# Neighbourhood attention: position biases added by VectorE together with the row maximum, instead of by matmuls with the identity

## The chip, the core and the metric

The kernel runs on one core of a Trainium2 chip. Its engines have a queue each: TensorE (PE in the profile; PEld is its weight load), VectorE (DVE), ScalarE (ACT), GpSimd (POOL) and SyncE (SP), which issues most of the DMA transfers. Each executes its own list of instructions in order and waits on semaphores for the others. The metric is the time of one execution on the device in microseconds (us); three runs of the kernel before took 1873.71, 1877.98 and 1898.75 us, so the median is 1877.98 us.

## The reference

Two network blocks run one after the other on 256 tokens of width 1024. The second block projects its input for three mixers (a gated linear recurrence, called hgrn in the code, a delta-rule recurrence, called rwkv, and a neighbourhood attention, called na), joins them by an output projection, and ends with a mixture of 32 experts. Only the attention is touched by the change. Cut to what matters, with 8 heads of 64 channels, 256 latent tokens on a grid of 4 rows by 64 columns, and 256 context tokens:

```python
s_win = jnp.einsum('bhjqd,bhrjkd->bhjqrk', q_row, k_blk) * scale
bias = rpb[:, row_idx[None, None, :, None], col_idx[:, :, None, :]]
s_win = jnp.where(in_win[:, :, None, :], s_win + bias, NEG_INF_2)
s_ctx = jnp.einsum('bhjqd,bhld->bhjql', q_row, kc_h) * scale
s_all = jnp.concatenate([s_win.reshape(s_win.shape[:4] + (n_win,)), s_ctx], axis=-1)
prob = jax.nn.softmax(s_all, axis=-1)
o = (jnp.einsum('bhjqrk,bhrjkd->bhjqd', p_win, v_blk)
     + jnp.einsum('bhjql,bhld->bhjqd', p_ctx, vc_h))
```

A query sees the latent keys in its window, with a bias by relative position, and all context keys without one. The softmax runs over both together.

## The kernel before, in words

The attention of the latent tokens is `na_lat`. It goes in eight steps (j, i): j is one of four pairs of heads, i one of two halves of the 256 queries. The two heads of a pair lie in rows 0 to 63 and 64 to 127 of the tiles `q`, `k` and `kc`, so that a matmul of one head uses half of the array's rows (64*128 in the profile). For each step and head (`par`) a PSUM tile `sj` of 128 queries by 512 keys is made: 256 latent keys (L1478) and 256 context keys (L1481). The pool of `sj` has two buffers (`LPS`, L25), which the projections before the attention use too.

The bias of a head, window mask included, was prepared much earlier in device memory (`na_table`). `na_bias` (L1403) loads it with four strided transfers on SP's queue (L1409) into a tile `nab`, of which there are two, so that the tile of head n is that of head n+2. It is added in PSUM by a matmul with the identity as the stationary operand and the bias as the moving one (L1475), ahead of the head's own matmuls. Then DVE takes the negative maximum of the 512 sums (L1485), ACT the exponentials with their sum (L1487), DVE the reciprocal (L1488), ACT the scaling (L1489). `flip` transposes the probabilities on PE (L1498) and ACT copies them out (L1499); after both halves of a pair, `values` multiplies them with the values (L1510, L1512).

The work around it is written as generators, taken in turns by `lat_mix` (L1576): the end of hgrn (L1007 scores, L1062 to L1069 read-out), two groups of rwkv (L1229 to L1366, among them the rounds L1289, L1290, L1294, L1296, L1298, L1299 between PE and DVE), and the attention. From what is written a scheduler in the compiler's front end sets the order of each engine by its own estimates, so that a change in one place moves instructions on several engines. SP's list in this part is: the loads `nkl` and `nvl` of the context keys and values, the biases of heads 0 to 3, four rows of the output projection `wo`, an expert weight, the biases of heads 4 to 7, and then the other expert weights (L1774), each into a buffer that older work has to give up. After the attention its pools are closed, and their space becomes expert buffers (L1624 to L1630). The output projection (L366 to L368 into `so`), the router and the 32 experts (L1928 to L1972) follow.

## Time and profile before

| | |
|---|---|
| runs | 1873.71, 1877.98, 1898.75 us; median 1877.98 us |
| the profiled execution | 1878.12 us, its span 1876.3 us |
| mean granted TensorE clock | 0.958 of full speed |
| busy share of the span | PE 92%, DVE 58%, ACT 37%, POOL 8% |
| matmuls with the identity (L1475) | 32 instructions, two for each of 16 tiles, between 1265.8 and 1360.3 us |
| attention of the latent tokens | from 1265.8 us to its last ACT copy at 1371.5 us |
| last stretch with experts | DMA engines at 425 GB/s from 1440 to 1860 us |

An f32 matmul of the program stands as two instructions in the trace. [...] The profile models the ends of matmuls, so a duration of one is its latency; what it takes of PE's time is read from the chain of waits, where each piece runs until the next one starts.

### The profile page before, as it was taken

The numbers are of one execution on the slowest core, as the hardware profiler recorded it, in microseconds if no ns is written. First come the engines' busy times: TensorE is split into PE (matmuls) and PEld (weight loads), VectorE is DVE, ScalarE is ACT, GpSimd is POOL, SyncE is SP. The second block draws the span as 40 slices with busy tenths as digits, with TensorE's granted clock in tenths as the row PEclk, the third lists the DMA queues.
The fourth block names the chain that finished last, engine by engine and source line by source line (L and its number), as shares of the span: only waits on it lengthen the run. The fifth ranks groups of instructions, "written<-read, shape, count | busy, mean of one in ns | idle before, by whom it ended". The sixth has DMA issues, their size and how long they took to land.

```text
span 1876.3 us, 37673 instructions
## 1 busy us (share of the span) xinstructions
PE 1726.2 (92%) x15846; PEld 1476.6 (79%) x15846; DVE 1096.1 (58%) x2087; ACT 691.3 (37%) x1078; POOL 149.5 (8%) x295
## 2 busy tenths in 40 slices
PE   7999999999989999999999978989988888887876
PEld 6879999999988889999999978976777555544443
DVE  5558578998645466689996589884544111111111
ACT  3356445654433355555553336422532000000000
POOL 2600000000220000000000001120001100101000
PEclk9999999999999999999999979975998999988999
DMA  9855555555677867444443433320349999999997
GB/s 311 250 205 165 169 192 186 190 175 214 211 226 266 289 226 224 150 166 146 159 157 124 149 146 124 113 68 12 113 187 373 428 429 427 429 429 428 429 428 290
DMA packets 94705, 441.14 MB, mean 235 GB/s; under 512 B 23796, under 2 KB 26388, under 8 KB 81728
## 3 DMA queue, kind: packets, MB, share of 16 engines
q1 hardware_dynamic: 90496, 432.17, 62.3%
q0 software_dynamic: 2224, 5.19, 1.2%
q8 instruction: 126, 2.06, 0.4%
q10 hardware_dynamic: 1808, 1.30, 0.2%
q14 instruction: 51, 0.42, 0.1%
HBM read 429.40 MB, written 9.20 MB: 234 GB/s over the span
## 4 chain that ended last, share of the span: by engine, by line
PE 55%; DMA 19%; DVE 7%; issue 2%; ACT 1%; POOL 1%; SPq 0%; ACTq 0%; POOLq 0%; DVEq 0%
PE g L366 8%; PE g L368 8%; PE g L367 8%; DMA we<-in_w_exp_up 6%; DMA we<-in_w_exp_gate 4%; DMA we<-in_w_exp_down 4%; PE g L1948 3%; PE acc L1972 2%; PE acc L368 2%; PE acc L366 2%; PE acc L367 2%; DVE wl L360 2%; DMA w<-in_w_in 1%; PE g L1965 1%; DMA z<-in_na_rpb 1%
## 5 line engine op out<-in xcount | busy, mean ns | idle before, releaser
L360 DVE TENSOR_TENSOR wl<-w,wh 128x1024 fp32r<-128x1024 f32 x347 | 429.2, 1238 | 234.9 <-ACT wh L359 230.4
L359 ACT ACTIVATE wh<-w 128x1024 fp32r<-128x1024 f32 x347 | 366.7, 1059 | 476.8 <-PE g L367 214.0
L366 PE MATMUL g<-xg,wh 128*128 128x256 f32 x1472 | 417.6, 284 | 13.2 <-ACT wh L359 13.2
L368 PE MATMUL g<-xg,wl 128*128 128x256 f32 x1472 | 416.8, 283 | 4.1 <-DVE wl L360 3.8
L367 PE MATMUL g<-xg,wh 128*128 128x256 f32 x1472 | 414.1, 281 | 0.0
L366 PEld LDWEIGHTS g<-xg,wh 128*128 128x128 f32 x1472 | 279.7, 190 | 19.8 <-ACT wh L359 13.8
L368 PEld LDWEIGHTS g<-xg,wl 128*128 128x128 f32 x1472 | 279.6, 190 | 13.8 <-DVE wl L360 5.8
L367 PEld LDWEIGHTS g<-xg,wh 128*128 128x128 f32 x1472 | 279.9, 190 | 4.2 <-issue 2.7
L1948 PEld LDWEIGHTS g<-we,xt 128*32 128x32 f32 x4096 | 109.9, 110 | 42.1 <-issue 27.9
L1948 PE MATMUL g<-we,xt 128*32 128x128 f32 x4096 | 125.9, 274 | 11.7 <-DMA we<-in_w_exp_up 11.7
L1954 DVE SCALAR_TENSOR_TENSOR hd<-hd,g 128x128 f32<-128x128 f32 x32 | 9.2, 288 | 214.0 <-ACT hd L1953 214.0
L1972 PE MATMUL acc<-dn,S 128*128 128x512 f32 (+1 forms) x264 | 123.2, 600 | 0.0
L1969 DVE TENSOR_TENSOR dn<-g,g2r 128x512 f32<-128x512 f32 (+1 forms) x66 | 44.6, 676 | 92.4 <-PE g L1965 90.2
L1965 PE MATMUL g<-we,ht 128*32 128x512 f32 (+1 forms) x528 | 71.4, 663 | 25.4 <-DMA we<-in_w_exp_down 16.7
L1953 ACT ACTIVATE hd<-g 128x128 f32<-128x128 f32 x32 | 8.9, 277 | 209.9 <-PE g L1948 209.9
L1972 PEld LDWEIGHTS acc<-dn,S 128*128 128x128 f32 x264 | 48.0, 197 | 43.4 <-issue 42.0
L1937 POOL TENSOR_SCALAR gr<-G,comb 128x128 f32<-128x128 f32 x64 | 38.1, 606 | 495.1 <-PE g L1941 351.9
L1943 ACT ACTIVATE S<-g 128x256 f32<-128x256 f32 x32 | 12.3, 384 | 156.2 <-PE g L1941 156.2
L366 PE MATMUL sj<-hl,wh 128*128 128x256 f32 x200 | 58.5, 292 | 6.8 <-ACT wh L359 5.7
L368 PE MATMUL sj<-hl,wl 128*128 128x256 f32 x200 | 57.8, 290 | 1.5 <-DVE wl L360 1.5
L367 PE MATMUL sj<-hl,wh 128*128 128x256 f32 x200 | 58.4, 292 | 0.1
L1965 PEld LDWEIGHTS g<-we,ht 128*32 128x32 f32 x528 | 15.9, 117 | 53.3 <-issue 37.4
(803 smaller groups left out, 3604.6 us busy)
## 6 DMA issues: line engine op xcount, KB each, us to landing
w<-in_w_in SPq DMA_DIRECT2D x135, 512.0 KB, 3.5
we<-in_w_exp_gate SPq DMA_DIRECT2D x32, 2048.0 KB, 37.3
we<-in_w_exp_up SPq DMA_DIRECT2D x32, 2048.0 KB, 38.4
we<-in_w_exp_down SPq DMA_DIRECT2D x31, 2048.0 KB, 34.3
w<-in_w_up SPq DMA_DIRECT2D x88, 512.0 KB, 3.3
wa<-in_w_ada SPq DMA_DIRECT2D x48, 512.0 KB, 4.9
w<-in_w_down SPq DMA_DIRECT2D x44, 512.0 KB, 3.3
w<-in_w_v SPq DMA_DIRECT2D x24, 512.0 KB, 3.4
```

The costliest lines, as they stand in the source:

```text
L359: s.nc.scalar.activation(hi, t, AF.Copy)
L360: s.nc.vector.tensor_tensor(lo, t, hi, op=OP.subtract)
L366: mm(out, w[0], x[0], start=first, stop=False, skip_group_check=sk)
L367: mm(out, w[0], x[1], start=False, stop=False, skip_group_check=sk)
L368: mm(out, w[1], x[0], start=False, stop=last, skip_group_check=sk)
L1937: nc.gpsimd.tensor_scalar(gr[:, i], G[:, i, e % 4, None, :].to_broadcast([128, 4, 32]), s.comb[:, i, e:e + 1], None, op0=OP.mult)
L1943: nc.scalar.activation(S, p[:, :T], AF.Copy)
L1948: nc.tensor.matmul(p[32 * j:32 * j + 32, q * 128:(q + 1) * 128], xt[:, k, (e % 4) * 32:(e % 4) * 32 + 32], w[:, k, j * 128:(j + 1) * 128], ...
L1954: nc.vector.scalar_tensor_tensor(hd[:, 0], hd[:, 0], 1.0, p[:, 0:128], op0=OP.add, op1=OP.mult)
L1965: nc.tensor.matmul(p[32 * c:32 * c + 32, :w], ht[:, c * 32:(c + 1) * 32], wd[:, c, q * w:(q + 1) * w], start=True, stop=True, tile_positio ...
L1969: nc.vector.tensor_tensor(dn, p[:, :w], s.g2r[:, q * w:(q + 1) * w], op=OP.mult)
L1972: nc.tensor.matmul(y[i][q * w // 512][:, o:o + w], S[:, i * 128:(i + 1) * 128], dn, start=(more and e == 0), stop=(e == 31), skip_group_ch ...
```

## The change

The bias tile gets three parts of 256 columns: bias of the first query half, zeros (a memset on POOL), bias of the second half. A step of the first half reads parts 0 and 1, a step of the second half parts 1 and 2; so for the second half the context keys are put ahead of the latent ones in PSUM, and the transposes pick their columns accordingly. The identity matmuls are gone. In their place the former maximum becomes one DVE operation that reads PSUM and the bias, writes the negative sum to the SBUF tile `e`, and keeps its minimum. ACT takes the exponentials from `e` instead of from PSUM. The bias loads are issued for both heads of a pair ahead of any matmul of the step, and the matmuls are written so that the two heads alternate.

```diff
--- before.py
+++ after.py
@@ -1401,12 +1401,14 @@
                 yield
 
     def na_bias(s, hd, pp):
-        b = pp.tile([128, 2, T], F32, name="nab", tag="nab", bufs=2)
+
+        b = pp.tile([128, 3, T], F32, name="nab", tag="nab", bufs=2)
+        s.nc.gpsimd.memset(b[:, 1], 0.0)
         base = s.nasc
         for qr in range(4):
             src = bass.AP(tensor=base.tensor, offset=base.offset + hd * 64 * 889 + (3 - qr) * 127 + 63,
                           ap=[[888, 64], [127, 4], [1, 64]])
-            s.nc.sync.dma_start(b[(qr % 2) * 64:(qr % 2) * 64 + 64, qr // 2].rearrange("p (r c) -> p r c", r=4), src)
+            s.nc.sync.dma_start(b[(qr % 2) * 64:(qr % 2) * 64 + 64, qr // 2 * 2].rearrange("p (r c) -> p r c", r=4), src)
         return b
 
     def na_qk(s, h, t0, gain, mul, rope, out):
@@ -1469,22 +1471,21 @@
             i0 = slice(i * 128, (i + 1) * 128)
             ps = [s.psj() for _ in range(2)]
             for par in range(2):
-                hd = 2 * j + par
                 if i == 0:
-                    nab[hd] = s.na_bias(hd, pp)
-                nc.tensor.matmul(ps[par][:, :T], s.ident, nab[hd][:, i], start=True, stop=False, skip_group_check=True)
+                    nab[2 * j + par] = s.na_bias(2 * j + par, pp)
+
+            for x, c in ((k, i), (kc, 1 - i)):
+                for par in range(2):
+                    r = half(par)
+                    nc.tensor.matmul(ps[par][:, c * T:c * T + T], q[r, j, i0], x[r, j], start=True, stop=True,
+                                     skip_group_check=True)
             for par in range(2):
-                r = half(par)
-                nc.tensor.matmul(ps[par][:, :T], q[r, j, i0], k[r, j], start=False, stop=True, skip_group_check=True)
-            for par in range(2):
-                r = half(par)
-                nc.tensor.matmul(ps[par][:, T:], q[r, j, i0], kc[r, j], start=False, stop=True, skip_group_check=True)
-            for par in range(2):
-                p = ps[par]
                 st = pp.tile([128, 4], F32, name="st", tag="st", bufs=2)
-                nc.vector.tensor_reduce(st[:, 0:1], p, axis=AX.X, op=OP.max, negate=True)
                 e = pp.tile([128, 512], F32, name="e", tag="e", bufs=3)
-                nc.scalar.activation(e, p, AF.Exp, bias=st[:, 0:1], accum_out=st[:, 1:2])
+
+                nc.vector.tensor_tensor_reduce(e, ps[par], nab[2 * j + par][:, i:i + 2].rearrange("p a t -> p (a t)"),
+                                               -1.0, 3e38, OP.add, OP.min, accum_out=st[:, 0:1])
+                nc.scalar.activation(e, e, AF.Exp, scale=-1.0, bias=st[:, 0:1], accum_out=st[:, 1:2])
                 nc.vector.reciprocal(st[:, 2:3], st[:, 1:2])
                 nc.scalar.activation(e, e, AF.Copy, scale=st[:, 2:3])
                 es[par, i] = e
@@ -1495,7 +1496,8 @@
                 pts[2 * j + par] = pp.tile([128, 4, T], F32, name="npt", tag="npt", bufs=3)
             p = s.ps2()
             for c in range(4):
-                nc.tensor.transpose(p[:, c * 128:(c + 1) * 128], e[:, c * 128:(c + 1) * 128], s.ident)
+                o = (c ^ 2 * i) * 128
+                nc.tensor.transpose(p[:, c * 128:(c + 1) * 128], e[:, o:o + 128], s.ident)
             nc.scalar.activation(pts[2 * j + par][:, :, i * 128:(i + 1) * 128], p.rearrange("p (c t) -> p c t", c=4),
                                  AF.Copy)
 
```

On each engine the order changes from the start of the attention to the output projection. The memsets stand on POOL as eight instructions: two before the last `hxs` and `hxp`, one ahead of the two `rgml` memsets, five behind them. SP's list is the same.

PE, the start of the attention (`nab` with `small` is the identity matmul; `nk` and `nkl` are the latent and the context keys, `hT` the queries; `rZl`, `rU` belong to rwkv, `ql` and `ye` to hgrn). Before:

```order
L1314 MATMUL sr<-rvtl,rgml_13362 128x64 x2
L901 MATMUL sx<-small,ye 128x128 x4
L1007 MATMUL sx<-ql,kl 128x128 x8
L1325 MATMUL sr<-rZl_14077,rRl_13459 128x64 x2
L1325 MATMUL sr<-rZl_14087,rRl_13471 128x64 x2
L1007 MATMUL sx<-ql,kl 128x128 x4
L1331 MATMUL sr<-rU1l_14302,rgml_13351 128x64 x2
L1007 MATMUL sx<-ql,kl 128x128 x4
L1331 MATMUL sr<-rU0l_14308,rgml_13362 128x64 x2
L1475 MATMUL sj<-nab,small 128x256
L1478 MATMUL sj<-nk,hT 128x256
L1481 MATMUL sj<-nkl,hT 128x256
```

Now:

```order
L1314 MATMUL sr<-rvtl,rgml_13362 128x64 x2
L1480 MATMUL sj<-nk,hT 128x256 x2
L901 MATMUL sx<-small,ye 128x128 x4
L1007 MATMUL sx<-ql,kl 128x128 x8
L1325 MATMUL sr<-rZl_14077,rRl_13459 128x64 x2
L1480 MATMUL sj<-nkl,hT 128x256 x2
L1325 MATMUL sr<-rZl_14087,rRl_13471 128x64 x2
L1007 MATMUL sx<-ql,kl 128x128 x4
L1331 MATMUL sr<-rU1l_14302,rgml_13351 128x64 x2
L1007 MATMUL sx<-ql,kl 128x128 x4
L1331 MATMUL sr<-rU0l_14308,rgml_13362 128x64 x2
```

The latent keys' matmuls of the first two heads now stand next to each other and ahead of L901, which waits for `ye`; the context keys' follow together, and no bias stands between them.

PE, the end of the first pair (`rbrl` is rwkv's, L1062 to L1069 the read-out of hgrn, L1498 and L1500 the transposes of the attention). Before:

```order
L1360 MATMUL sr<-rgml_13362,rU0l_14308 64x128
L1478 MATMUL sj<-nk,hT 128x256
L1481 MATMUL sj<-nkl,hT 128x256
L1062 MATMUL sx<-hf_13113,hS_115 128x256
L1251 MATMUL sr<-rbrl_14500,ranl_14501 128x256 x2
L1498 MATMUL sx<-small,e 128x128 x3
L1063 MATMUL sx<-hf_13114,hS_116 128x256
L1069 MATMUL sx<-hsc,hv 64x128
L1069 MATMUL sx<-hxc_14851,hv 64x128
```

Now:

```order
L1360 MATMUL sr<-rgml_13362,rU0l_14308 64x128
L1480 MATMUL sj<-nk,hT 128x256
L1480 MATMUL sj<-nkl,hT 128x256
L1251 MATMUL sr<-rbrl_14500,ranl_14501 128x256 x4
L1062 MATMUL sx<-hf_13113,hS_115 128x256
L1500 MATMUL sx<-small,e 128x128 x4
L1063 MATMUL sx<-hf_13114,hS_116 128x256
L1069 MATMUL sx<-hsc,hv 64x128
L1069 MATMUL sx<-hxc_14849,hv 64x128
```

The key matmuls of head 2 (L1480 at the top) have come ahead of L1251 and L1062, behind which they stood before, and four L1251 now stand in a row.

DVE, from the second half of the third pair to the first half of the last (`rTl`, `rRl`, `rY5l` are rwkv's). Before:

```order
L1485 TENSOR_REDUCE st<-sj 128x1
L1298 TENSOR_TENSOR rTl_14702<-sr,rTl_14702 128x16x16
L1299 TENSOR_TENSOR rRl_14670<-sr,rRl_14670 128x16x16
L1488 RECIPROCAL st<-st 128x1
L1485 TENSOR_REDUCE st<-sj 128x1
L1290 TENSOR_TENSOR rY5l_15109<-sr,consts_79 128x512
L1488 RECIPROCAL st<-st 128x1
L1290 TENSOR_TENSOR rY5l_15116<-sr,consts_79 128x512
L1485 TENSOR_REDUCE st<-sj 128x1
L1298 TENSOR_TENSOR rTl_14695<-sr,rTl_14695 128x8x32
L1299 TENSOR_TENSOR rRl_14658<-sr,rRl_14658 128x8x32
L1488 RECIPROCAL st<-st 128x1
```

Now:

```order
L1486 ISA e,st<-sj,nab 128x512
L1486 ISA st 128x1
L1298 TENSOR_TENSOR rTl_14702<-sr,rTl_14702 128x16x16
L1299 TENSOR_TENSOR rRl_14670<-sr,rRl_14670 128x16x16
L1489 RECIPROCAL st<-st 128x1
L1290 TENSOR_TENSOR rY5l_15105<-sr,consts_79 128x512
L1486 ISA e,st<-sj,nab 128x512
L1486 ISA st 128x1
L1486 ISA e,st<-sj,nab 128x512
L1486 ISA st 128x1
L1290 TENSOR_TENSOR rY5l_15112<-sr,consts_79 128x512
L1489 RECIPROCAL st<-st 128x1
```

Each maximum is now the new operation with the bias as an operand, followed by a row that reads its minimum out. Those of head 5's second half and head 6's first half (the second and third L1486 with an input) now stand next to each other.

## Rows read from the trace of the kernel before

**Rows 1.** The page, part 1: busy time, share of the span, instructions

```profile
PE 1726.2 (92%) x15846; PEld 1476.6 (79%) x15846; DVE 1096.1 (58%) x2087; ACT 691.3 (37%) x1078; POOL 149.5 (8%) x295
```

**Rows 2.** Windows: length, busy time (instructions) per engine, PEclk, DMA share, GB/s

```profile
1256.40:1307.60 51.20, 51.20 (x176) 35.92 (x174) 23.63 (x51) 8.39 (x19) 4.90 (x4) 0.50 0.18 41
1307.60:1372.00 64.40, 64.03 (x415) 47.13 (x415) 34.21 (x87) 32.55 (x70) 0.00 (x0) 1.00 0.27 82
1372.00:1400.00 28.00, 27.74 (x229) 25.51 (x228) 13.66 (x35) 8.61 (x14) 0.00 (x0) 1.00 0.53 200
1400.00:1440.00 40.00, 30.43 (x302) 29.38 (x306) 24.11 (x100) 10.76 (x26) 3.81 (x6) 0.79 0.89 375
1440.00:1860.00 420.00, 348.55 (x5057) 203.86 (x5045) 73.37 (x150) 29.08 (x93) 34.25 (x58) 0.96 1.00 425
```

**Rows 3.** The chain of waits by line, the two stretches of rows 2

```profile
by line: PE sx L1007 24.2%; PE sr L1251 16.5%; PE sx L1069 9.0%; PE sj L1475 8.6%; PE sj L1478 8.2%; PE sj L1481 6.2%; PE sx L1062 4.5%; PE sr L1331 4.1%; PE sr L1360 4.0%; PE sx L1063 3.3%; PE sr L1356 2.6%; PE sr L1359 2.5%; PE sr L1336 2
...
by line: PE sx L1510 15.7%; PE sj L1478 11.6%; PE sx L1498 11.4%; PE sj L1475 9.4%; PE sr L1289 9.3%; PE sj L1481 8.6%; PE sr L1296 8.4%; PE sr L1294 7.4%; PE sr L1251 5.1%; PE sr L1331 1.8%; PE sx L1069 1.8%; PE sr L1262 1.7%; PE sx L882 1
```

**Rows 4.** The chain in order of time: start, length (us), what

```profile
1267.11 1.15 PE sj L1478 x2
1268.26 0.85 PE sj L1481 x2
...
1323.85 0.63 PE sj L1478 x2
1324.47 0.43 PE sj L1481 x2
```

**Rows 5.** Timelines of ACT and PE: start, length, instruction [idle before it <-releaser]

```profile
1251.88 1.06 ACT L1436 ACTIVATE nv<-sj 128x512 f32<-128x512 f32 x2
...
1256.13 0.92 PE L901 MATMUL sx<-small,ye 128*128 128x128 f32 x4 [2.87 <-DVE ye L896]
...
1280.54 0.79 PE L1478 MATMUL sj<-nk,hT 64*128 64x256 f32 x1
1280.55 0.79 PE L1007 MATMUL sx<-ql,kl 64*128 64x128 f32 x2
...
1305.42 1.06 PE L1063 MATMUL sx<-hf,hS 128*128 128x256 f32 x2
```

**Rows 6.** A window of PE alone: length, busy time (instructions), PEclk, DMA

```profile
1225.00:1230.00 5.00, 4.70 (x24) 0.57 0.00 0
```

**Rows 7.** Groups by line: xcount, busy us, mean ns, idle before

```profile
L1485 DVE TENSOR_REDUCE st<-sj 128x1 f32<-128x512 f32 x16 | 11.1, 692 | 15.8 <-PE sj L1481 13.4 <-ACT rtml L1263 1.0 <-ACT e L1489 0.8
L1487 ACT ACTIVATE e<-sj,st 128x512 f32<-128x512 f32 x16 | 10.9, 684 | 19.5 <-DVE st L1485 16.5 <-PE sx L1498 3.0
L1487 ACT ACTIVATION_READ_ACCUMULATOR e<-sj,st 128x1 f32 x16 | 3.1, 195 | 0.0
L1299 DVE TENSOR_TENSOR rRl<-sr,rRl 128x256 fp32r<-128x256 f32 x12 | 5.0, 416 | 2.2 <-PE sr L1296 2.2
L1290 DVE TENSOR_TENSOR rY6l<-sr,consts 128x512 fp32r<-128x512 f32 x2 | 1.4, 692 | 1.6 <-PE sr L1289 1.6
...
L559 DVE SCALAR_TENSOR_TENSOR e<-acc,bias 128x512 f32<-128x512 f32 x16 | 11.0, 687 | 4.0 <-PE acc L557 3.8
...
L562 ACT ACTIVATE e<-e,st 128x512 f32<-128x512 f32 x16 | 11.5, 719 | 11.0 <-DVE st L561 10.9
...
L360 DVE TENSOR_TENSOR wl<-w,wh 128x1024 fp32r<-128x1024 f32 x347 | 429.2, 1238 | 234.9 <-ACT wh L359 230.4
...
L1047 POOL MEMSET hxs<- 128x256 f32 x1 | 0.3, 331 | 0.0
```

**Rows 8.** The bias loads: ns min/median/max, first and last start; landing

```profile
L1409 SPq DMA_DIRECT2D nab<-nasc x32: 573/617/1681, 1255.2 to 1349.7; - x32
...
DMA to landing us min/median/max: 2.3/2.5/10.2
```

**Rows 9.** Waits of SP's queue, 1200 to 1480: us, times, longest

```profile
SPq L1774 <- PE sx L1510: 19.2, 1, 19.2
```

## The prediction, made before the changed kernel had run

> **What bounds the kernel now.** I read the page first: TensorE (PE) is busy for 92% of the span [rows 1], but that is a mean over stages, so the stage of the change has to be read by itself. The windows by stage [rows 2] give it. From 1256.4 to 1372 us, the attention with the ends of hgrn and rwkv, PE has no gap to speak of (51.20 of 51.20 us, then 64.03 of 64.40), while DVE is busy for 23.63 and 34.21 us and ACT for 8.39 and 32.55. The chain of waits [rows 3] runs through PE's matmuls in both stretches. So PE bounds the stage, and PE work that leaves it should shorten it.

> [...] The clock fell after PE had waited 2.87 us for `ye` before L901 [rows 5] and came back when matmuls over all 128 rows (L1062, L1063) ran one behind the other [rows 5].

> Behind the stage, SP's next expert load waits 19.2 us for the attention's last matmuls (L1510) [rows 9], the output projection again keeps PE full (27.74 of 28.00 us), and from 1440 to 1860 us the DMA engines are at a share of 1.00 with 425 GB/s [rows 2]. All of this hangs on the end of the attention, and none of its transfers gets shorter or can start earlier by itself, so I take a microsecond gained at 1372 us as one gained at the end.

> **The change part by part.** *Identity matmuls.* There are 16 (32 instructions), 4 in the slow stretch, 12 in the fast one. In the chain they hold 8.6% of 51.2 us = 4.4 us and 9.4% of 64.4 us = 6.05 us [rows 3]. Gone: **-10.4 us**.

> *The first key matmuls.* The latent keys' pair of heads 0 and 1 now stands ahead of L901, in PE's wait of 2.87 us. Their `sj` buffers are free by then: ACT's last copies out of them end at 1251.88 + 1.06 = 1252.94 us, and PE's wait begins at 1256.13 - 2.87 = 1253.26 us [rows 5]. So the pair costs nothing there, where before it took 1.15 us for each head [rows 4] (the second head's pieces in the chain are as long). The context pair follows with both heads next to each other; matmuls in different halves of the rows run side by side (L1478 and L1007 start at 1280.54 and 1280.55 and both take 0.79 us [rows 5]). So I give the pair 1.15 us in place of 2 x 0.85. Together 4.0 us become 1.15: **-2.85 us**.

> *Head 2's keys* move from the fast into the slow stretch, by the order of PE: 1.15 + 0.85 = 2.0 us instead of 0.63 + 0.43 = 1.06 [rows 4]: **+0.9 us**.

> *DVE.* The maximum takes 692 ns. The trace has no operation that adds two tensors and keeps an extremum. The nearest is L559, which reads a PSUM tile and an SBUF tile of the same 128x512 and writes one: 687 ns. The dearest reading is two passes' worth, the 1238 ns of L360 over 1024 elements [rows 7]. I take 0.69 us, since L559 has the same operands, and keep 1.24 for the range. The read-out row costs between nothing and ACT's counterpart of 195 ns [rows 7]; I take 0.1 us, 1.6 us in all. DVE has 28 and 30 us free in the two stretches [rows 2], which hide it.

> *ACT.* The exponentials read SBUF now. 719 ns (L562) in place of 684 ns (L1487) [rows 7] is 16 x 0.035 = 0.6 us on an engine that is half idle: nothing. That `sj` is given up one ACT operation earlier is worth nothing either, as PE's list shows no gap in which it waited for it [rows 2].

> *POOL.* Eight memsets of 128x256, 0.33 us each [rows 7], on an engine that is busy for 4.90 us in the slow stretch and not at all in the fast one [rows 2]. One stands ahead of the `rgml` memsets, which wait for PE's L1360 later than it waits for DVE: nothing. Were that cover gone, 0.33 us would show. The other columns of the transposes and the 2 KB more of SBUF per partition move no work.

> *The new wait.* A bias buffer was free after a matmul early in a step; now it is free after DVE's operation, and DVE itself waits for the next bias. From the release, four issues at 0.617 us and a landing of 2.5 us [rows 8] make 5.0 us. For head 6, DVE's list leaves between the release (head 4, second half) and the use only L1298, L1299, L1290 and head 5's operation: 0.42 + 0.42 + 0.69 + 0.69 = 2.2 us [rows 7]. So DVE may stand 2.8 us, and for head 7 as long again. Queued behind it on DVE are rwkv's L1290, L1298 and L1299, for which PE's L1294 and L1289 wait. PE has other work in its list there, and some of DVE's time is waiting for PE anyway; between 0 and 5.6 us I take half, **+3 us**. [...]

> *The clock.* Each microsecond by which the slow stretch ends sooner, at equal work, is half a microsecond. The L1251 now come as four in a row, and L1062, L1500 and L1063 behind them, all three over 128 rows, as a closer block than before; the clock may come back there, up to 10 us sooner. That is 0 to -5 us; I take -1.

> **Sum:** -10.4 - 2.85 + 0.9 + 3 - 1 = -10.3 us from the profiled execution's 1878.1 us, which is within 0.2 us of the median: **1868 us**. With the waits at 0 to 5.6 us and the clock at -5 to 0, the forecast's own range is 1861 to 1872.

> **Rivals.** *The clock does not fall at all* (chance 0.10). The key pair fills about 1 us of the gap after which it fell. For it: the fall is tied to that gap. Against: 1.8 us of it remain, and at 1225 to 1230 us the clock fell to 0.57 although PE was busy 4.70 of 5.00 us [rows 6]. It would give back up to half of 51.2 us, but DVE's 23.63 us [rows 2] then bound the stretch nearly as tightly as PE's 25; taking half to nine tenths of it, 13 to 22 us, the time is 1846 to 1856 us.

> *The new operation is slow, or DVE's waits take the gain* (0.17). The stage's bound goes over to the head's own path from matmul through DVE and ACT to the transposes. Without waits and clock the sum is -12.35 us; with all 5.6 us of waiting, and between nothing and all of the 16 x 0.55 = 8.8 us that an operation of 1.24 us adds on DVE, the time is 1871 to 1880 us. For it speaks that the rwkv rounds share DVE's queue; against it that PE had work on hand throughout. [...]

> *The clock stays low for longer* (0.12), the case on the slow side. What leaves are matmuls over all 128 rows; what stays of the heads' first part is 64*128, half of the array. Rows 6 show that the clock can fall while PE is busy, so a stage with less full-width work can be slow for longer, or again. [...] Against it: with a large part of 64-row work in the mix the clock held at 1.00 from 1307.6 to 1400 us [rows 2].

> *It does not do what it says*: PE's time is not given back because something else ends last behind the attention, as the tail of rwkv. Then nothing changes, 1876 to 1880 us; I put it in with the second rival, whose time it shares, and leave 0.03 for what I have not seen.

> **Numbers.** The forecast has 0.58. It and the second rival span 1861 to 1880; with the upper part of the first and the lower part of the third the range is **1855 to 1884 us**, a little over 0.8. A change of 2%, about what a measurement of this kernel can tell from none, is 37.6 us, to 1840 or 1916 us. Faster than that takes the first rival with all of its 25 us and no new wait: 0.03. Slower takes the third at more than its worst, 0.04. Within: 0.93.

> **What would show it.** Right: PE still without gaps from the first key matmuls on, no L1475, and the stretch up to the attention's last copy shorter by some 10 us, with the experts following at the same rate. The operation at about 0.69 us on DVE with a short read-out behind it. DVE waiting for DMA of `nab` in front of the new operation for heads 6 and 7, for less than 3 us each. The granted clock falling near 1256 us and back at 1.00 between 1290 and 1307 us. Wrong: a PE that waits for DVE in the rwkv rounds (second rival), or a clock of 0.50 behind 1310 us (third), or of 1.00 from 1253 us on (first).

## The result, and the profile after

Five runs of the changed kernel against five of the kernel before: median 1859.8 us against 1878.7 us, a ratio of 0.9896 with an interval of 0.9866 to 0.9926, so 14 to 25 us less. In a second series, on one chip, it was 1858.9 us (six runs) against 1875.9 us, ratio 0.9889 (0.9854 to 0.9925). The forecast was 1868 us; the time lies in its range, below the forecast's own part of 1861 to 1872. One execution in the first series ran all through at a granted clock of 0.71 to 0.76 (mean 0.735) and took 2165.7 us; it is the one that was profiled there, so the profile after is that of the second series, of an execution of 1859.2 us.

The page, part 1, and the windows by stage, to be held against [rows 1] and [rows 2]; the attention is cut where the granted clock changes (PEclk, the column behind the busy times, as a share of full speed), apart from a second stretch at 0.50, from 1308.8 to 1312.2 us, which lies in the fourth window:

```profile
PE 1700.9 (92%) x15814; PEld 1467.7 (79%) x15814; DVE 1093.2 (59%) x2103; ACT 692.1 (37%) x1078; POOL 153.5 (8%) x303
```

```profile
1262.80:1267.80 5.00, 2.77 (x27) 2.13 (x28) 4.86 (x16) 1.91 (x5) 0.28 (x2) 0.99 0.52 165
1267.80:1288.30 20.50, 20.19 (x96) 16.56 (x94) 13.44 (x37) 5.06 (x12) 1.60 (x3) 0.50 0.30 72
1288.30:1308.80 20.50, 19.87 (x145) 16.02 (x145) 16.13 (x43) 8.24 (x17) 3.86 (x3) 1.00 0.09 18
1308.80:1351.60 42.80, 42.80 (x297) 33.53 (x296) 25.37 (x73) 28.04 (x61) 1.25 (x4) 0.96 0.40 124
1351.60:1380.00 28.40, 28.18 (x236) 26.26 (x236) 13.99 (x36) 8.92 (x15) 0.00 (x0) 1.00 0.50 191
1380.00:1420.00 40.00, 30.16 (x283) 29.12 (x287) 24.14 (x100) 10.77 (x26) 3.81 (x6) 0.79 0.89 378
1420.00:1840.00 420.00, 345.43 (x5044) 203.65 (x5039) 73.30 (x150) 29.07 (x93) 34.25 (x58) 0.97 1.00 425
```

TensorE has 32 instructions fewer and still hardly a gap (20.19 of 20.50, then 19.87 of 20.50 and 42.80 of 42.80 us): it remains the bound, as before. The stretch at 0.50 is 20.50 us long and no longer 51.20. The rest of the program is as it was: 28.40 us of output projection, 40 us of transition, the experts at 425 GB/s.

**From mark to mark.** I count the attention from the last ACT copy of `nv` (1252.4 us before, 1262.8 us after) to ACT's last copy of the output (1371.5 and 1351.6 us). Both are starts of the copies. Before: 119.1 us, of which 51.2 at 0.50. After: 88.8 us, of which 20.5 + 3.4 = 23.9 at 0.50. From there to the first matmul with an expert's weights it is 65.5 and 65.9 us, and from there to the end 439.3 and 439.5. So a microsecond at the end of the attention is one at the end of the program, as the prediction had it. The 30.3 us show as only 19 in the span because this execution came to the mark 10.4 us later. The work ahead of the mark is the same, and over twelve profiles its time lies anywhere from 1252.4 to 1262.8 us, whatever the kernel.

To take the clock out I count a microsecond at 0.50 as half of one (one head's keys, by [rows 4], take 2.00 us at 0.50 and 1.06 us at 1.00). The attention's **work** is then 119.1 - 25.6 = 93.5 us before and 88.8 - 11.95 = 76.9 us after. It is a rough measure, since not all slows down with TensorE's clock (in the change's profile DVE's new operation takes 669 to 693 ns throughout, at 0.50 as at 1.00); the table below gives it for each kernel.

**The new operation.** Groups by line (DVE and ACT), and then the lines' own views: minimum, median and maximum in ns, and for whom the engine waited (us, times):

```profile
L1486 DVE DVE_READ_ACCUMULATOR2_ANT st<- x16: 78/83/85, 1272.8 to 1343.7; 128x1 f32 x16
...
  DMA nab<-nasc: 1.7, 2
...
L1406 POOL MEMSET nab<- x8: 311/312/313, 1262.5 to 1334.3; 128x256 f32 x8
...
L1411 SPq DMA_DIRECT2D nab<-nasc x32: 573/610/1355, 1265.6 to 1336.8; - x32
```

The operation takes 686 ns on the mean, as L559 did (687 ns in [rows 7]), and its read-out 83 ns. DVE waited for biases twice, 1.7 us in all. The exponential from SBUF takes 720 ns, as predicted from L562.

**The chain and the gap.** The chain of waits over the attention, then PE's timeline at its beginning (an f32 matmul is two instructions, so x4 is a pair of matmuls):

```profile
by line: PE sj L1480 16.4%; PE sx L1512 11.0%; PE sx L1007 10.0%; PE sx L1500 9.7%; PE sr L1289 6.9%; PE sr L1296 5.9%; DMA nkl<-nkv 5.9%; PE sr L1294 5.7%; PE sr L1251 5.4%; PE sx L1069 3.7%; PE sr L1331 2.6%; PE sx L1062 1.4%; issue 1.4%;
...
1269.72 1.23 PE sj L1480 x4
...
1313.58 1.07 PE sj L1480 x8
...
1320.12 1.06 PE sj L1480 x4
```

```profile
1263.67 0.70 PE L1480 MATMUL sj<-nk,hT 64*128 64x256 f32 x4
1266.61 0.66 PE L901 MATMUL sx<-small,ye 128*128 128x128 f32 x4 [2.23 <-DVE ye L896]
1267.19 1.65 PE L1007 MATMUL sx<-ql,kl 64*128 64x128 f32 x16
```

Four things are to be seen. No identity matmul is left. The latent keys' pair of heads 0 and 1 stands in front of L901, at no cost, and the wait there is 2.23 us instead of 2.87 [rows 5]. The context keys' pair behind it (1269.72) has come so early that it waits for their load, `nkl`; that is why the chain has 5.9% of it, but TensorE's own wait there is only 0.31 us. And in two places (1313.58, and again at 1330.11) *both* heads' four key matmuls, x8, take the 1.07 us that one head's pair takes otherwise (x4, 1.06 us, the same as the 0.63 + 0.43 us of [rows 4]): with no identity matmul between them the two heads, which lie in different halves of the rows, run side by side, 8 instructions in 1.07 us.

SP's expert load behind the attention still waits for it, less long than in [rows 9]:

```profile
SPq L1776 <- PE sx L1512: 12.1, 1, 12.1
```

### The profile page after: what moved, and what is told of

Read it like the earlier page. It is cut to its first block, busy times and chain, and to the rows that moved or that the text cites. A ratio compares the mean times of both kernels' runs of the same rounds, so it can differ in the third digit from the quotient of the medians.

```text
span 2163.5 us, 37642 instructions
## 1 busy us (share of the span) xinstructions
PE 2064.4 (95%) x15814; PEld 1742.4 (81%) x15814; DVE 1106.1 (51%) x2103; ACT 692.6 (32%) x1078; POOL 148.5 (7%) x303
## 4 chain that ended last, share of the span: by engine, by line
PE 78%; DVE 4%; DMA 2%; ACT 1%; issue 1%; ACTq 0%; DVEq 0%
PE g L368 10%; PE g L366 10%; PE g L367 9%; PE g L1950 7%; PE acc L1974 6%; PE g L1967 4%; PE acc L366 3%; PE acc L367 3%; PE acc L368 3%; PE g L1930 2%; PE sj L366 2%; PE sj L367 1%; PE sj L368 1%; DMA we<-in_w_exp_up 1%; PE acc L849 1%; PE sj L1480 1%
## 5 line engine op out<-in xcount | busy, mean ns | idle before, releaser
L360 DVE TENSOR_TENSOR wl<-w,wh 128x1024 fp32r<-128x1024 f32 x347 | 428.0, 1234 | 326.3 <-ACT wh L359 315.9
L366 PE MATMUL g<-xg,wh 128*128 128x256 f32 x1472 | 468.7, 319 | 12.7 <-ACT wh L359 12.7
L368 PE MATMUL g<-xg,wl 128*128 128x256 f32 x1472 | 466.3, 317 | 1.9 <-DVE wl L360 1.9
L367 PE MATMUL g<-xg,wh 128*128 128x256 f32 x1472 | 460.4, 313 | 0.0
L366 PEld LDWEIGHTS g<-xg,wh 128*128 128x128 f32 x1472 | 329.0, 224 | 21.0 <-ACT wh L359 13.4
L368 PEld LDWEIGHTS g<-xg,wl 128*128 128x128 f32 x1472 | 326.2, 222 | 12.4 <-issue 6.1
L367 PEld LDWEIGHTS g<-xg,wh 128*128 128x128 f32 x1472 | 328.5, 223 | 4.6 <-issue 3.3
L1950 PEld LDWEIGHTS g<-we,xt 128*32 128x32 f32 x4096 | 131.1, 124 | 46.4 <-issue 32.0
L1950 PE MATMUL g<-we,xt 128*32 128x128 f32 x4096 | 156.3, 319 | 0.0
L1974 PE MATMUL acc<-dn,S 128*128 128x512 f32 (+1 forms) x264 | 155.5, 736 | 0.0
L1967 PE MATMUL g<-we,ht 128*32 128x512 f32 (+1 forms) x528 | 84.8, 776 | 13.6 <-ACT ht L1961 12.7
L366 PE MATMUL sj<-hl,wh 128*128 128x256 f32 x200 | 65.7, 328 | 3.0 <-ACT wh L359 1.9
L367 PE MATMUL sj<-hl,wh 128*128 128x256 f32 x200 | 65.9, 329 | 0.1
L367 PE MATMUL acc<-hidqk,wh 128*128 128x256 f32 x192 | 60.3, 315 | 0.0
## 6 DMA issues: line engine op xcount, KB each, us to landing
we<-in_w_exp_up SPq DMA_DIRECT2D x32, 2048.0 KB, 13.2
```

The lines of the kernel that those rows point to most:

```text
L360: s.nc.vector.tensor_tensor(lo, t, hi, op=OP.subtract)
L366: mm(out, w[0], x[0], start=first, stop=False, skip_group_check=sk)
L367: mm(out, w[0], x[1], start=False, stop=False, skip_group_check=sk)
L368: mm(out, w[1], x[0], start=False, stop=last, skip_group_check=sk)
L1950: nc.tensor.matmul(p[32 * j:32 * j + 32, q * 128:(q + 1) * 128], xt[:, k, (e % 4) * 32:(e % 4) * 32 + 32], w[:, k, j * 128:(j + 1) * 128], ...
L1967: nc.tensor.matmul(p[32 * c:32 * c + 32, :w], ht[:, c * 32:(c + 1) * 32], wd[:, c, q * w:(q + 1) * w], start=True, stop=True, tile_positio ...
```

## Experiments

All ran with the kernel before beside them on the same chip; ratios are to it. Theory A: TensorE's time that left (identity matmuls, key matmuls side by side) is the gain, and what lies beyond it is TensorE's clock. Its rivals: the order alone, the new operation, or the clock alone. The diffs below leave out the start and stop flags of the neighbouring matmuls, which follow from each edit.

**1. The change again, and the identity matmuls back.** The second of these adds the part of the bias tile that is zero, so nothing but TensorE's work, and the order that the scheduler makes of it, differs from the change.

```diff
+            for par in range(2):
+                nc.tensor.matmul(ps[par][:, i * T:i * T + T], s.ident, nab[2 * j + par][:, 1], start=True, stop=False,
+                                 skip_group_check=True)
```

> The changed kernel once more, for a profile at the usual clock. Theory A (PE's time of the identity matmuls and of the first key pair): PE still without gaps; the part of the stage before the experts is some 12 us shorter in PE work, and the rest of the measured 19 us must then be the clock coming back sooner, by 10 to 15 us. Theory B (the filled gap keeps the clock up): no stretch at 0.50 begins near 1256 us at all. Theory C (order only): the gain lies elsewhere than between 1253 and 1372 us. Time 1853 to 1861 us.

> The change with the 16 identity matmuls put back on PE; they add the zeros of the bias tile's middle part, so that the output is the same, and VectorE's operation stays. Theory A: 8 to 11 us slower than the change, about 1868 us. Theory B or C (clock or order alone): within 3 us of the change, about 1859 us, since the order and VectorE's work are the change's.

Measured: 1858.9 us (0.9889, 0.9854 to 0.9925), and 1859.2 us with the identity back (0.9909, 0.9878 to 0.9939). Taken by the time alone this contradicts theory A: 16 identity matmuls more cost nothing. The window over the attention and PE's timeline at its beginning, of the kernel with the identity back:

```profile
1256.40:1347.50 91.10, 88.88 (x580) 65.92 (x580) 58.88 (x163) 42.72 (x91) 7.31 (x12) 1.00 0.30 88
```

```profile
1259.01 0.70 PE L1483 MATMUL sj<-nk,hT 64*128 64x256 f32 x2
1260.20 0.66 PE L901 MATMUL sx<-small,ye 128*128 128x128 f32 x4 [0.49 <-DVE ye L896]
```

The clock stays at 1.00 all through in this execution, one of the quicker (1854.7 us). The attention's work is 91.1 us, 14 more than in the change, and the 12 us that the change loses to its 23.9 us at half speed aren't lost here. Two effects of nearly the same size cancel; the other runs bear it out (below the table). In front of L901 TensorE waits for only 0.49 us, since the identity matmuls of heads 0 and 1 stand in that gap.

**2. The order alone**, in the kernel before: all key matmuls first, the two heads in turn, then the identity matmuls with the biases.

```diff
-                nc.tensor.matmul(ps[par][:, :T], s.ident, nab[hd][:, i], start=True, stop=False, skip_group_check=True)
...
+            for par in range(2):
+                nc.tensor.matmul(ps[par][:, :T], s.ident, nab[2 * j + par][:, i], start=False, stop=True,
+                                 skip_group_check=True)
```

> The kernel before with one thing of the change: the key matmuls of a step come first and alternate between the heads, and the identity matmul with the bias comes last into the same PSUM tile. Theory A: only the first key pair is gained, 2 to 3 us, so 1874 to 1877 us. Theory C (the place of the key matmuls in front of L901 and the clock behind it are the gain): 1860 to 1866 us.

Measured: 1877.2 us, ratio 1.0013 (0.9984 to 1.0043). The order alone gives nothing that the time shows. In the profile (of the quickest run, 1872.4 us) its attention is 113.5 us with 44.4 at 0.50, so its work is 91.3 us, 2.2 less than before, which is what theory A gives the first key pair. In its timeline the first keys of heads 0 and 1 run side by side (x4 in 0.70 us at 1254.46 and in 1.23 us at 1260.86), but those at 1276.15 are one head's alone (x2 in 1.22 us, then x2 in 1.06 us).

**3. The operation in two**, an addition and a maximum (the exponentials then need no change of sign):

```diff
-                nc.vector.tensor_tensor_reduce(e, ps[par], nab[2 * j + par][:, i:i + 2].rearrange("p a t -> p (a t)"),
-                                               -1.0, 3e38, OP.add, OP.min, accum_out=st[:, 0:1])
+                nc.vector.tensor_tensor(e, ps[par], nab[2 * j + par][:, i:i + 2].rearrange("p a t -> p (a t)"), op=OP.add)
+                nc.vector.tensor_reduce(st[:, 0:1], e, axis=AX.X, op=OP.max, negate=True)
```

> The change with its VectorE operation split in two: an addition into SBUF and a maximum over the 512 sums, about 0.69 us more on VectorE for each of 16 tiles, 11 us in all. Theory A (VectorE has room, PE bounds the stage): 0 to 4 us slower than the change, 1858 to 1864 us. Rival (VectorE's waits already bound the heads' path): 8 to 11 us slower, about 1869 us.

Measured: 1864.7 us (0.9933, 0.9896 to 0.9969), 6 us above the change, though the runs of both overlap (1851 to 1878 against 1853 to 1863). The groups by line of DVE:

```profile
L1487 DVE TENSOR_REDUCE st<-e 128x1 f32<-128x512 f32 x16 | 10.9, 680 | 0.3
L1486 DVE TENSOR_TENSOR e<-sj,nab 128x512 f32<-128x512 f32 x16 | 10.9, 684 | 4.3 <-PE sx L1500 1.5 <-DMA nab<-nasc 1.3 <-issue 0.8
```

10.9 us more on DVE cost at most about 6. Most of that goes with the clock: its runs at a mean granted clock of 0.954 to 0.956 took 1869 to 1878 us, those at 0.960 to 0.967 took 1851 to 1866. Its work is 80.3 us against 76.9. Adding and reducing in one operation is worth between nothing and 6 us here.

**4. No bias at all**: the kernel before with its identity matmuls left out and nothing in their place (the biases are not added).

```diff
-                nc.tensor.matmul(ps[par][:, :T], s.ident, nab[hd][:, i], start=True, stop=False, skip_group_check=True)
```

> The kernel before with the 16 identity matmuls left out and nothing in their place: the biases are loaded but added nowhere, and the maximum is taken as before. It has TensorE's saving without the new VectorE operation. Theory A (the new operation costs nothing over the old maximum, and VectorE hardly waits for the biases): the same as the change within 3 us, 1856 to 1862 us. Rival (the new operation's wait or length costs the 3 us of the prediction's sum or more): 1852 to 1856 us, that is faster than the change by 3 us or more.

Measured: 1861.1 us (0.9893, 0.9848 to 0.9937), not faster than the change. Work 79.1 us, 30.7 us at 0.50. So the new operation, its read-out and its wait for biases cost nothing that can be seen; the +3 us of the prediction are not there.

**5. Filling the gap in front of L901**, in the change and in the kernel before, with four matmuls of the identity in the first step:

```diff
+            if (j, i) == (0, 0):
+                for par in range(2):
+                    for c in range(2):
+                        nc.tensor.matmul(ps[par][:, c * T:c * T + T], s.ident, k[:, 0], start=True, stop=True,
+                                         skip_group_check=True)
```

> The change, with four more matmuls of the identity (all 128 rows, 256 columns, about 0.43 us each) in front of the first step's key matmuls, on parts of the sums that the key matmuls then overwrite: they fill the 2.2 us in which TensorE waits before L901. Theory A (TensorE's time goes with the identity matmuls, and what came beyond it is the clock, which depends on how TensorE is busy when the attention begins): the attention is granted 1.00 nearly throughout, where the change's profile had 23.9 us at half speed; about 12 us less for 0.5 to 1 us more work: 1846 to 1852 us. Rival (the clock falls whatever stands in that gap): 1858 to 1861 us, a low stretch of 20 us or more stays in the attention.

> The kernel before, with the same four matmuls at the same place. Theory A: the clock is a matter of the work at the attention's start and not of the change: the low stretch of 51.2 us goes or shrinks, by up to 25.6 us: 1851 to 1862 us. Against the change with the same four matmuls it stays 8 to 13 us behind where the clocks are alike, since the identity matmuls still stand on TensorE. Rival (the clock falls whatever stands in that gap): 1875 to 1879 us.

Measured: 1859.8 us (0.9891, 0.9840 to 0.9941) and 1877.3 us (0.9987, 0.9959 to 1.0016). In both theory A missed: the time is where its rival put it. The windows of the filled change, cut where its clock changes, say why:

```profile
1254.20:1292.90 38.70, 36.56 (x261) 28.46 (x260) 32.74 (x91) 15.30 (x33) 5.57 (x7) 1.00 0.28 69
1292.90:1299.70 6.80, 6.80 (x33) 6.56 (x33) 5.48 (x15) 3.10 (x8) 0.00 (x0) 0.51 0.32 103
1299.70:1320.20 20.50, 20.50 (x138) 15.14 (x138) 10.91 (x32) 11.22 (x23) 0.94 (x3) 1.00 0.59 198
1320.20:1344.10 23.90, 23.90 (x84) 17.07 (x83) 8.39 (x24) 10.15 (x22) 0.31 (x1) 0.50 0.11 22
```

The fall at the attention's beginning is gone, as theory A has it, but the clock fell twice later, for 30.7 us together, while PE was busy for every one of them. In the kernel before the gap only moved: the first identity matmul with a bias had now to wait for its load, from 1267.8 to 1269.9 us, and in that wait the clock fell, at 1268.8 us (PE's timeline):

```profile
1264.37 0.66 PE L901 MATMUL sx<-small,ye 128*128 128x128 f32 x4 [1.07 <-DVE ye L896]
...
1269.94 1.22 PE L1480 MATMUL sj<-nab,small 128*128 128x256 f32 x2 [2.17 <-DMA nab<-nasc]
```

**6. The identity back for two heads only**, of heads 0 and 1, then of heads 2 and 3:

```diff
+            for par in range(2):
+                if j == 0:    # the second kernel: j == 1
+                    nc.tensor.matmul(ps[par][:, i * T:i * T + T], s.ident, nab[par][:, 1], start=True, stop=False,
+                                     skip_group_check=True)
```

> The change with the identity matmuls put back for the first two heads alone (4 of 16, adding the part of the bias tile that is zero). Theory A: 4 x 0.43 us of TensorE more than the change, and the clock held over the first steps as in the kernel with all 16: 1846 to 1853 us, less than with all 16 (1859) and less than the change. Rival (only identity matmuls all along hold the clock): a low stretch of 20 us or more in the attention, 1859 to 1863 us.

> The change with the identity matmuls put back for heads 2 and 3 alone (4 of 16), in place of heads 0 and 1. Theory A (the clock is decided in the first 10 us of the attention, where heads 0 and 1 stand): the clock falls at L1007 as in the change, about 20 us at 0.50; with the four matmuls' 3.3 us, part of it in the slow stretch, 1859 to 1865 us. Rival (it is enough that some such matmuls stand anywhere in the attention): little or no low stretch, 1845 to 1852 us.

Measured: **1846.3 us** for heads 0 and 1 (six runs, 1844.7 to 1849.7; 0.9820, 0.9777 to 0.9864), the fastest kernel of all, and 1867.3 us for heads 2 and 3 (0.9942, 0.9918 to 0.9965). With the first the clock never falls in the attention, with the second it falls at L901 and there are 41.0 us at 0.50. So four matmuls that compute nothing go with 13 us less than the change's median in one place, and with 8 more in another (13 and 10 by the ratios, since the chips differ). The window over the attention with heads 0 and 1, and PE's timeline in front of L901; behind them the same timeline with heads 2 and 3:

```profile
1257.60:1338.80 81.20, 79.38 (x561) 61.31 (x561) 57.92 (x164) 42.59 (x92) 7.21 (x11) 1.00 0.34 98
```

```profile
1260.13 0.70 PE L1484 MATMUL sj<-nk,hT 64*128 64x256 f32 x2
1261.31 0.66 PE L901 MATMUL sx<-small,ye 128*128 128x128 f32 x4 [0.49 <-DVE ye L896]
...
1264.64 0.70 PE L1484 MATMUL sj<-nkl,hT 64*128 64x256 f32 x4 [1.02 <-DMA nkl<-nkv]
```

```profile
1257.19 0.70 PE L1484 MATMUL sj<-nk,hT 64*128 64x256 f32 x4
1260.13 0.87 PE L901 MATMUL sx<-small,ye 128*128 128x128 f32 x4 [2.23 <-DVE ye L896]
```

This kernel and the one with all 16 identity matmuls both run their attention at 1.00 throughout, so they give the cost of 12 identity matmuls without the clock: 91.1 - 81.2 = 9.9 us. The chains of waits by line, all 16 and then four, and pieces of the second chain:

```profile
by line: PE sj L1483 17.0%; PE sx L1515 10.9%; PE sx L1503 8.8%; PE sj L1478 8.1%; PE sr L1251 8.0%; PE sr L1289 6.3%; DMA nkl<-nkv 6.1%; PE sr L1296 5.9%; PE sr L1294 5.1%; PE sx L1007 5.1%; PE sx L1069 4.3%; PE sx L1062 1.4%; issue 1.4%; 
```

```profile
by line: PE sj L1484 14.3%; PE sx L1516 11.4%; PE sx L1504 9.8%; PE sr L1251 9.7%; PE sr L1289 7.4%; DMA nkl<-nkv 6.7%; PE sr L1296 6.5%; PE sr L1294 5.8%; PE sx L1007 5.7%; PE sx L1069 5.2%; PE sx L1062 1.6%; PE sj L1479 1.5%; PE sr L1331 
...
1302.04 1.07 PE sj L1484 x8
...
1317.92 1.07 PE sj L1484 x8
...
1324.39 1.07 PE sj L1484 x8
```

The identity matmuls (L1478, L1479) go from 8.1% of 91.1 = 7.4 us to 1.5% of 81.2 = 1.2 us, and the key matmuls (L1483, L1484) from 17.0% = 15.5 us to 14.3% = 11.6 us. So some 6 of the 9.9 us are the identity matmuls themselves, and some 4 the key matmuls. Three times both heads' keys take one head's 1.07 us (x8), which no piece of the chain with all 16 does; that is 3.2 of the 3.9 us.

**7. Rows or gap.** The same as with heads 0 and 1, but with identity matmuls of 64 rows; then with three of them for each head in the first step.

```diff
-                    nc.tensor.matmul(ps[par][:, i * T:i * T + T], s.ident, nab[par][:, 1], start=True, stop=False,
-                                     skip_group_check=True)
+                for n in range((3, 1)[i] if j == 0 else 0):    # the first of the two kernels: once
+                    nc.tensor.matmul(ps[par][:, i * T:i * T + T], s.ident[half(par)], nab[par][half(par), 1],
+                                     start=(n == 0), stop=False, skip_group_check=True)
```

> As the kernel with the identity matmuls back for heads 0 and 1 (1846 us, no low stretch in the attention), in the same order on TensorE and with matmuls of the same length, but each over 64 of the 128 rows (half of the identity, half of the bias tile's zero part). Theory A (it is the full rows of those matmuls that keep the clock up): the clock falls as in the change, 20 us or more at 0.50 in the attention, 1857 to 1864 us. Rival (that TensorE is occupied there, with whatever rows, or that the order of the work is another, decides): no low stretch, 1845 to 1850 us.

> As the kernel with half-row identity matmuls for heads 0 and 1 (64 rows each, those of the two heads side by side), but with three of them for each head in the first step, so that TensorE's wait before L901, 1.79 us there and 0.49 us with full rows, shrinks by about 1.3 us. It separates two readings of that kernel's slow stretch. Reading 1 (the wait before L901 decides): no slow stretch in the first 20 us of the attention, 1846 to 1853 us. Reading 2 (matmuls over half the rows do not hold the clock, filled gap or not): 20 us or more at 0.50 from about the L1007 on, 1856 to 1862 us.

Measured: 1857.0 us (0.9914, 0.9883 to 0.9945) and 1858.9 us (0.9886, 0.9831 to 0.9941). The timelines of PE, first with one, then with three:

```profile
1260.58 0.71 PE L1479 MATMUL sj<-nab,small 64*128 64x256 f32 x4
1261.12 0.61 PE L1484 MATMUL sj<-nk,hT 64*128 64x256 f32 x4
1263.51 0.66 PE L901 MATMUL sx<-small,ye 128*128 128x128 f32 x4 [1.79 <-DVE ye L896]
```

```profile
1260.60 0.59 PE L1484 MATMUL sj<-nk,hT 64*128 64x256 f32 x2
1261.16 0.66 PE L901 MATMUL sx<-small,ye 128*128 128x128 f32 x4
```

The first of the two looked like a victory for full rows, since the clock fell. But the two heads' half-row matmuls ran side by side (x4 in 0.71 us, where two heads' full-row ones took 0.65 and 0.70 us one after the other), not one behind the other as I had assumed, and left a wait of 1.79 us. With three of them the wait is gone, and so is the fall: 1.00 from 1257.4 to 1309.2 us. Here the gap decides the early fall, not the rows (matmuls over 64 rows in both kernels: after 1.79 us the clock fell, without a wait it didn't). Then the clock fell at 1309.2 us, for 44.4 us, so by its time this kernel is in neither reading's favour alone: its six runs lie at 1848 to 1852 us (mean granted clock 0.963 to 0.967) and at 1866 to 1871 us (0.954 to 0.960), three each.

What stands there was the same in the fastest kernel, whose clock did not fall. Windows of the half-row kernel with the gap filled and then of the fastest, whose matmuls are the same from 1290.5 us (1291.3 in the fastest) to the fall, in the same order, 0.9 us later:

```profile
1300.00:1305.00 5.00, 5.00 (x38) 3.27 (x36) 3.80 (x13) 4.16 (x10) 0.31 (x1) 1.00 0.98 369
1305.00:1310.00 5.00, 5.00 (x32) 4.08 (x32) 2.37 (x7) 3.08 (x7) 0.31 (x1) 0.91 0.96 387
```

```profile
1300.00:1305.00 5.00, 5.00 (x40) 3.72 (x40) 4.27 (x14) 4.60 (x11) 0.31 (x1) 1.00 0.89 335
1305.00:1310.00 5.00, 5.00 (x37) 3.89 (x33) 2.02 (x7) 3.52 (x7) 0.31 (x1) 1.00 1.05 435
```

**All kernels in one table.** The wait is TensorE's in front of L901; "fell at" is the granted clock's first fall in the attention.

| kernel | wait, us | L901 at | fell at | us at 0.50 | work, us | median, us |
|---|---|---|---|---|---|---|
| before | 2.87 | 1256.1 | 1256.4 | 51.2 | 93.5 | 1875.3 to 1881.4 |
| order only | 2.24 | 1257.4 | 1257.6 | 44.4 | 91.3 | 1877.2 |
| before, gap filled | 1.07, then 2.17 for `nab` | 1264.4 | 1268.8 | 30.7 | 95.8 | 1877.3 |
| identity back | 0.49 | 1260.2 | never | 0 | 91.1 | 1859.2 |
| the change | 2.23 | 1266.6 | 1267.8 | 23.9 | 76.9 | 1858.9 |
| two operations | 2.22 | 1262.7 | 1263.9 | 34.1 | 80.3 | 1864.7 |
| no bias | 2.23 | 1264.9 | 1265.6 | 30.7 | 79.1 | 1861.1 |
| gap filled | 0 | 1258.2 | 1292.9 | 30.7 | 81.0 | 1859.8 |
| heads 0 and 1 | 0.49 | 1261.3 | never | 0 | 81.2 | 1846.3 |
| heads 2 and 3 | 2.23 | 1260.1 | 1260.4 | 41.0 | 83.0 | 1867.3 |
| half rows | 1.79 | 1263.5 | 1264.2 | 20.5 | 77.9 | 1857.0 |
| half rows, gap filled | 0 | 1261.2 | 1309.2 | 44.4 | 79.0 | 1858.9 |

Waits of TensorE for `nkl` follow three microseconds behind L901; those of 1.12 us (identity back) and 1.02 us (heads 0 and 1) were followed by no fall.

**The same split over all runs.** The table's work is that of one execution of each kernel. Every run has its span and its mean granted clock on record, and their product is roughly the time that it would take at full clock. On the mean of the series that the kernels of experiments 1 and 2 shared, it is 1802 us for the kernel before, 1800 with the order alone, 1800 with the identity back and 1788 for the change; what the clock adds to it over the whole program is 75, 78, 58 and 68 us. In the series of the fastest kernel it is 1801 before and 1789 with heads 0 and 1, and the clock adds 79 and 56 us. So the clock alone is not the change's gain: some 14 of its 21 us (of the means) are work and some 7 the clock. With the identity back it is 2 and 16, with heads 0 and 1 it is 12 and 23.

## Why the prediction was right, and where its terms were off

- **What bounds the stage, and that its gain passes to the end**: right. TensorE has hardly a gap after either, and the parts behind the attention keep their length in all twelve profiles (64.0 to 66.3 us to the experts, 438.8 to 439.9 us from there).
- **The work.** The kernels with 16 identity matmuls have 93.5, 91.3, 95.8 (with four more in the gap) and 91.1 us of work, those with none (the change, two operations, no bias) 76.9, 80.3 and 79.1: 92.9 and 78.8 on the mean, 14 us less. The direct comparison at full clock gives 9.9 us for 12, in proportion 13.2 us for 16; over all runs it is 12 to 14.
- **Identity matmuls, -10.4 us**: right. 6.2 us for 12 at full clock are 8.2 us for 16; the prediction's two parts, the 4.4 us of the slow stretch taken at half, come to 8.25.
- **First key matmuls, -2.85 us**: right in itself. The latent pair is in the gap, the context pair takes 1.23 us (expected 1.15). The step that failed is that the term stopped there: it had seen that matmuls in different halves run side by side, and priced it for the first step only. It happens twice more in the change (x8 in 1.07 us, where one head alone takes 1.06), about -2.1 us.
- **Head 2's keys, +0.9 us**: not to be seen. In the change they stand at 1289.39 us, behind the end of the slow stretch, and take 1.06 us (x4).
- **DVE's wait, +3 us**: wrong. 1.7 us of waiting, and nothing of it is to be seen in the time, since the kernel without biases isn't faster. For heads 6 and 7 DVE was expected to stand up to 2.8 us each; the two waits that there are last 1.0 us at most.
- **The operation at 0.69 us and its read-out at 0.1**: right, 686 and 83 ns. The second rival rested on waits of 5.6 us and an operation of up to 1.24 us, and so falls. ACT's 720 ns and POOL's 312 ns: right, and hidden.
- **The clock, -1 us**: too small. The changed kernel's profile had 23.9 us at 0.50 in place of 51.2, worth up to 13.6 us in that pair of profiles; over the runs, 17 to 19 us less in the medians less some 12 to 14 for the work leave 3 to 7, and the split over all runs gives 7. The clock came back at 1288.3 us, 20.5 us after its fall and not 51.2, inside L1360 and L1356, ahead of the block that I had named for it (L1251 to L1063), so that block is not what brought it back here.
- **Rivals.** The clock that does not fall did not come true for the change, in which 2.23 us of the gap remained, as the prediction's counter-argument had it; its 1846 to 1856 us are what the kernel with heads 0 and 1 took (1846.3 us), in which 0.49 us of that gap are left. Low for longer, or again: the change's profile fell a second time, at 1308.8 us, and so was at 0.50 behind 1310 us, but for 3.4 us only; two of its variants did so for 23.9 and 44.4 us, from 1320.2 and 1309.2 us. No run shows the longer time at 0.50 from which the range takes its 1884 us: in the attention the profile of the change's second series had 23.9 us of it and no variant's more than 44.4, against 51.2 before.
- **Luck.** The sum gave 10.3 us, the medians 17 to 19. A cost that did not appear (+3), pairs not priced (-2.1) and a clock taken too small all err to the same side. The time lies in the range because the first rival had widened its lower end, and that rival did not come true.

**Still open**: why the clock falls late (at 1292.9, 1320.2 and 1309.2 us in the variants, at 1308.8 us in the change). The two windows above are of the same sequence, and in one execution the clock holds 1.00, so TensorE's work in those windows alone does not tell. In four profiles (the change, order only, no bias, gap filled) TensorE waited 0.3 us in front of L1294, for DVE's L1290, in the change 2.1 us before its late fall; but with the identity back the same wait (0.29 us) was followed by none, and in the 10 us before the falls at 1320.2 and 1309.2 us TensorE had no wait of more than 0.25 us. No run here separates the rest. Nor is it shown that the fastest kernel will hold its clock always; one of its runs was profiled, and all six lie within 5 us.

## What to carry to other kernels

Before you take matmuls away from an engine that bounds a stage, look at what stands in its waits: here a wait of 1.8 to 2.9 us in front of one line was followed by a granted clock of 0.50 within 1.3 us of that line's start in all seven kernels that had it (one profile each), and where the wait there was 0.5 us or less the clock held at that place in all four. A matmul that computes nothing, put into such a wait, can return more than the matmuls cost whose removal was the aim: 13 us in the kernel with heads 0 and 1, against some 8 us for all 16 identity matmuls. It need not: in two other kernels with that wait filled (1859.8 and 1858.9 us) a later fall took it back. And price pairs: work that separated two matmuls of different row halves cost its own time and the overlap of its neighbours, here some 6 and some 4 of the 9.9 us for 12 identity matmuls.

## What was not expected of the hardware

- The clock stays down although TensorE is never idle: 44.40 of 44.40 us busy at 0.50 from 1309.2 us in the half-row kernel with the gap filled, 23.90 of 23.90 from 1320.2 us in the filled change.
- The add with a running minimum costs DVE no more than a plain addition or a plain maximum of the same tile (686, 684 and 680 ns).
